# Layer 0's modulation by pool groups on 32-column TensorE tiles, with the mixer in turned form

## The chip, the core and the metric

The kernel runs on one core of one Trainium2 chip. The metric is the device time of one execution in microseconds, the median of several runs. Engines are named as in the profile: PE (TensorE), PEld (its weight loads), DVE (VectorE), ACT (ScalarE), POOL (GpSimd), SP (SyncE, which issues most DMAs).

## What is computed

A decoder trunk of two layers on a sequence of 256 tokens and 2048 channels, all in float32. Layer 0 mixes by causal window means, layer 1 by attention; each layer ends in a gated FFN of 5632 hidden channels. Shift, scale and gate of each sub-layer come from a vector `c`, through `mod_w[i]` (2048 x 12288, 100 MB a layer). The part that the change touches, cut:

```python
shift_m, scale_m, gate_m, shift_f, scale_f, gate_f = jnp.split(silu(c) @ mod_w[0] + mod_b[0], 6, axis=-1)
h = rmsnorm(x, norm_mix[0]) * (1 + scale_m) + shift_m
for g, w in enumerate((2, 4, 8, 16)):           # four groups of 512 channels
    d_g = causal window mean over w tokens of h_g, less h_g
    y_g = d_g @ pool_w[0, g]                    # 512 x 512
x = x + gate_m * (y * pool_scale[0])
h = rmsnorm(x, norm_ffn[0]) * (1 + scale_f) + shift_f
x = x + gate_f * swiglu(h, ffn_gate[0], ffn_up[0], ffn_down[0])
```

## The kernel before

**Units.** Weights of the big products come as units of 512 x 512 (1 MB). `w_unit` loads one, ACT rounds it to a high part (line 368), DVE takes the low part (line 370), and PE multiplies high and low parts with the two parts of the hidden state (`proj_unit`, line 392). The product with `silu(c)` has a single row, so before it is done mostly on DVE: `Part.unit` loads 128 rows of 2048 columns (1 MB, rows of 8 KB) and adds them, scaled, to `acc` (line 183); `BlockPart.unit` does it for 512 columns of shift and of scale at once (two loads of 512 KB in pieces of 2 KB, line 219; sums at line 233). Sums over partitions are then made by PE.

**Front.** Before the first FFN product, layer 0 needs shift, scale and gate of the mixer whole (48 loads of 1 MB) and the first quarter of the FFN's shift and scale (16 loads of 512 KB), `x`, the band matrices and the four pool weights (1 MB each). The order is: shift of the mixer, scale of the mixer, and between them the window products of the normed stream (lines 716 to 728); then pool weights, gate, and the products with pool weights (`pool_product`, line 784). Of the gate's 16 row tiles five go to PE (`GM_PE`, line 200), the rest to DVE. Then `add_gated` adds the gated result to `x` (lines 525 and 526), the squares are summed over the free axis on ACT (line 410), POOL takes the power -0.5 of two columns (line 415), and the first quarter of the hidden state is scaled, turned by PE (line 444) and modulated (lines 458 to 460). Of the first block of the FFN's shift and scale half of the rows are summed on PE (line 230) and the rest on DVE, and PE folds them into columns (line 247).

**What sets the order.** The units of modulation lie in a list, `background`; `pump` emits the next ones. In the FFN one unit of weights is followed by a share of a unit of background. SP issues in the order of the program and waits for one of six `raw` buffers; each engine runs its instructions in order. The front from the modulation of the window means to the first hidden block stands in `manual_schedule`, so it runs as written; elsewhere a scheduler with priorities orders the instructions.

**First FFN.** `start_ffn` begins six chunks of gate and up block by block of the hidden state; blocks 1 to 3 are scaled on ACT (line 434), turned on PE and modulated while PE works on the block before. At chunk 5 the stream `x` is written to DRAM (`stream_aside`, 2 MB, line 482) and the tile gathers the FFN's sum.

Of the kernel before, what the change touches and what calls it, by code (L numbers as in the profile page):

```python
# [9 lines left out]
F32 = mybir.dt.float32  # L10
# [37 lines left out]
C_END = C_FOLD + P  # L48
# [9 lines left out]
GM_PE = (8, 10, 12, KD - 2, KD - 1)  # L58
# [8 lines left out]
V_NM, V_NF, V_KVIN, V_KVN, V_QN, V_C, V_END = 0, 32, 64, 80, 84, 88, 104  # L67


def shape_constants():  # L70
# [8 lines left out]
    con[:, C_SIGN] = np.where(q % ROPE < HALF, -1.0, 1.0)  # L79
    band = np.zeros((P, len(WINDOWS), BAND_W), np.float32)  # L80
# [12 lines left out]
def tile_trunk(ctx: ExitStack, tc: tile.TileContext, a: dict, out: bass.AP):  # L93
# [34 lines left out]
    # constants and small vectors  # L128
    x = const.tile([P, NT, D], F32, name="x")

    def load_x(tok):
        sync.dma_start(x[:, tok, :], a["x"][0, tok * P:(tok + 1) * P, :])
# [22 lines left out]
    sync.dma_start(vrows[V_QN:V_QN + 4], a["q_norm"].rearrange("l (r q) -> (l r) q", q=P))  # L155
    vps = ps_t()
    pe.transpose(vps[:, :V_END], vrows, ident[:V_END, :V_END])
    vcol = const.tile([P, V_C], F32, name="vcol")
    dve.tensor_copy(vcol, vps[:, :V_C])
# [3 lines left out]
    # adaLN rows: acc[p, n] = sum over row tiles of w[kt*128+p, n] * silu(c); partition 0 starts at the bias  # L163
# [22 lines left out]
    # a gate on all partitions, with some of its row tiles summed on the idle tensor engine  # L186
    class SharedPart(Part):
        def add(self, r):
            if self.kt == 0:
                self.banks = [ps_t() for _ in range(ND)]  # L190
            if self.kt not in GM_PE:
                super().add(r)
                return
            rep = t2k([P, P])
            act.activation(rep, ones, AF.Copy, scale=s_col[:, self.kt:self.kt + 1])
            for j in range(ND):
                js = slice(j * CH, (j + 1) * CH)
                if self.kt == KD - 1:
                    pe.matmul(self.banks[j], lhsT=ones, rhs=self.acc[:, js], start=False, stop=False)
                pe.matmul(self.banks[j], lhsT=rep, rhs=r[:, js], start=self.kt == GM_PE[0], stop=self.kt == KD - 1)  # L200

    # the same for CH columns of shift and scale at once, two row tiles in a unit
    class BlockPart:
        def __init__(self, w, b, col, done, shared):
            self.w, self.b, self.col, self.done, self.shared, self.kt = w, b, col, done, shared, 0
            self.banks = None

        def unit(self):
            pick = slice(self.col, self.col + CH)
            if self.kt == 0:  # L210
                self.acc = work.tile([P, 2, CH], F32, tag="acc", bufs=2, name=nm("acc"))
                pool.memset(self.acc, 0.0)
                sync.dma_start(self.acc[0:1], self.b.rearrange("o (i n) -> o i n", i=2)[:, :, pick])
                if self.shared:
                    self.banks = [ps_t() for _ in range(2)]
# [4 lines left out]
            if self.shared and self.kt == KD - 2:  # L220
                self.sums = ps_t()
                for i in range(2):
                    row = t2k([P, CH])
                    act.activation(row[0:1, :], self.banks[i][0:1, :], AF.Copy)
                    self.add_sums(i, row[0:1, :], ones[0:1, 0:1], i == 0, False)
            for k in range(2):
                s_ = s_col[:, self.kt + k:self.kt + k + 1]
                if self.shared and k == 1 and self.kt < KD - 2:
                    for i in range(2):
                        pe.matmul(self.banks[i][0:1, :], lhsT=s_, rhs=r[:, k, i, :], start=self.kt == 0,  # L230
                                  stop=self.kt == KD - 4)
                else:
                    dve.scalar_tensor_tensor(out=self.acc, in0=r[:, k], scalar=s_, in1=self.acc,  # L233
                                             op0=ALU.mult, op1=ALU.add)
            self.kt += 2
            if self.kt == KD and self.shared:
                for i in range(2):
                    self.add_sums(i, self.acc[:, i], ones[:, 0:1], False, i == 1)
                self.done(self.sums)
            elif self.kt == KD:  # L240
                self.done(self.acc)

        def add_sums(self, i, rows, ones_, first, last):
            """Adds the sums over partitions of rows [..., CH] to KL columns of a bank, which only its first product clears."""
            for k in range(KL):
                n = i * KL + k
                pe.matmul(self.sums[:, n:n + 1], lhsT=rows[:, k * P:(k + 1) * P], rhs=ones_, start=first and k == 0,
                          stop=last and k == KL - 1)
# [3 lines left out]
    def folded(acc, n, fin):  # L252
        """Sums over partitions of acc [P, n]: column 32 * b + i is in row 32 * r + i of column b, for any r."""
# [17 lines left out]
    def to_cols(fin):  # L271
        def done(acc):
            pt = ps_t()
            for j in range(KD):
                pe.matmul(pt[:, j:j + 1], lhsT=acc[:, j * P:(j + 1) * P], rhs=ones[:, 0:1], start=True, stop=True)  # L275
            fin(pt[:, :KD], slice(0, P))
        return done

    def shift_to(i, form=to_cols_folded):
        return form(lambda pt, rows: dve.tensor_copy(cols[rows, i, :], pt))  # L280

    def scale_to(i, g, form=to_cols_folded):
        return form(lambda pt, rows: dve.scalar_tensor_tensor(
# [42 lines left out]
    # units of the background for a unit of weights  # L326
# [4 lines left out]
    def hold():  # L331
        """Emit no more of the background until release()."""
# [14 lines left out]
    def plan(left, units):  # L347
        """Spread the background down to what is left over the next units of weights."""
# [4 lines left out]
    # what follows a unit of weights, queued behind the split of the next unit, which is more pressing  # L353
# [9 lines left out]
    # weights: a unit of 512 rows and 512 columns, split exactly into two parts of 12 bits  # L363
# [23 lines left out]
    def proj_unit(banks, t_, hi, lo, first, last, toks=range(NT)):  # L387
        """Adds a unit to the banks; the products with the lower part of the weights, which is split last, come last."""
# [13 lines left out]
    # statistics of the residual stream  # L402
# [5 lines left out]
    def stat_piece(tok, j):  # L408
        junk = work.tile([P, CH], BF16, tag="junk", bufs=1, name=nm("junk"))
        act.activation(junk, x[:, tok, j * CH:(j + 1) * CH], AF.Square, accum_out=ssq[0][:, tok, j:j + 1])  # L410
# [68 lines left out]
    def stream_aside(l):  # L479
        aside[l] = dram.tile([P, NT, D], F32, name=nm("aside"))  # L480
# [53 lines left out]
    # a projection of the hidden state, begun before all of the hidden state is known  # L534
# [109 lines left out]
    # rope tables with the rows of two heads on partitions; the sine has the sign of its half  # L644
# [32 lines left out]
    def rope_start(bank):  # L677
        """bank [128, T] holds the rows of two heads; returns what rope_end needs."""
# [13 lines left out]
    rope_tables()  # L692
    load_x(1)
    band = hl_t([P, len(WINDOWS), BAND_W], F32)
    sync.dma_start(band, a["band"].rearrange("p (g n) -> p g n", g=len(WINDOWS)))
    psc = hl_t([P, D], F32)
    ps_row = t2k([P, CH])
    for j in range(ND):
        sync.dma_start(ps_row[j * 32:j * 32 + 1, :], a["pool_scale"][0:1, j * CH:(j + 1) * CH])
    for j in range(ND):  # L700
        pt = ps_t()
        pe.matmul(pt, lhsT=ones[j * 32:j * 32 + 1, :], rhs=ps_row[j * 32:j * 32 + 1, :], start=True, stop=True)
        act.activation(psc[:, j * CH:(j + 1) * CH], pt, AF.Copy)
    stat_start()
    for tok in range(NT):
# [413 lines left out]
```

## Time and profile before

| what | us |
|---|---|
| median of 3 runs | 1964.37 (1963.92 to 1965.63) |
| span of the profiled execution | 1962.3 |
| last loads of the front have landed (66.3 MB) | about 172.7 |
| first product of the first FFN | 184.3 |
| PE busy in the whole span | 1853.0 |

The profile comes from one profiled execution; its span runs from the first to the last instruction, and the time of a run holds what lies around it too. The profile's views give, for a stretch, the busy time of each engine and how many instructions it ran; for a group, the count, the busy time, the mean length of one and the idle time ahead of it; for DMA, the bytes and the rate.

### The profile page before, as it was taken

The numbers are of one execution on the slowest core, as the hardware profiler recorded it, in microseconds if no ns is written. First come the engines' busy times: TensorE is split into PE (matmuls) and PEld (weight loads), VectorE is DVE, ScalarE is ACT, GpSimd is POOL, SyncE is SP. The second block draws the span as 40 slices with busy tenths as digits, with TensorE's granted clock in tenths as the row PEclk, the third lists the DMA queues.
The fourth block names the chain that finished last, engine by engine and source line by source line (L and its number), as shares of the span: only waits on it lengthen the run. The fifth ranks groups of instructions, "written<-read, shape, count | busy, mean of one in ns | idle before, by whom it ended". The sixth has DMA issues, their size and how long they took to land. (4 is left out here: it accounts for less than half of the span.)

```text
span 1962.3 us, 21516 instructions
## 1 busy us (share of the span) xinstructions
PE 1853.0 (94%) x8485; PEld 1520.7 (77%) x8485; DVE 1546.4 (79%) x1312; ACT 850.0 (43%) x939; POOL 35.9 (2%) x33
## 2 busy tenths in 40 slices
PE   0489999999999999998999999999999999999998
PEld 0444888888888888886789987888888888888886
DVE  7887899998778778888989975889986566554556
ACT  3123544444443333334676744544444433343333
POOL 1000000000000000000000000000000000000000
PEclk9889999999999999999899999999999999999999
DMA  9999998898898989987888684989887667665561
GB/s 377 408 378 365 379 321 305 310 350 327 313 329 302 332 325 345 338 333 284 307 311 304 228 295 142 360 303 325 297 293 260 225 229 257 235 209 186 195 219 70
DMA packets 225184, 572.66 MB, mean 292 GB/s; under 512 B 11958, under 2 KB 16286, under 8 KB 203442
## 3 DMA queue, kind: packets, MB, share of 16 engines
q1 hardware_dynamic: 225084, 571.30, 80.9%
q8 instruction: 66, 1.08, 0.2%
q14 instruction: 34, 0.28, 0.0%
HBM read 564.97 MB, written 6.29 MB: 291 GB/s over the span
## 5 line engine op out<-in xcount | busy, mean ns | idle before, releaser
L392 PE MATMUL ps<-hl,act 128*128 128x512 f32 x7008 | 1609.5, 391 | 4.7 <-ACT act L459 2.2
L392 PEld LDWEIGHTS ps<-hl,act 128*128 128x128 f32 x7008 | 1315.1, 188 | 279.3 <-ACT act L459 4.4
L370 DVE TENSOR_TENSOR hl<-raw,hl 128x2048 fp32r<-128x2048 f32 x296 | 676.2, 2289 | 239.9 <-ACT hl L368 236.1
L368 ACT ACTIVATE hl<-raw 128x2048 fp32r<-128x2048 f32 x296 | 566.4, 1919 | 608.7 <-PE ps L392 542.1
L183 DVE SCALAR_TENSOR_TENSOR acc<-raw,s_col,acc 128x2048 f32<-128x2048 f32 x155 | 364.0, 2348 | 4.2 <-DMA raw<-in_mod_w_dram 1.6
L233 DVE SCALAR_TENSOR_TENSOR acc<-raw,s_col,acc 128x1024 f32<-128x1024 f32 x121 | 155.0, 1281 | 8.7 <-DMA raw<-in_mod_w_dram 7.2
L556 DVE TENSOR_TENSOR act<-ps,act 128x512 f32<-128x512 f32 x96 | 64.6, 687 | 14.1 <-PE ps L392 13.7
L275 PE MATMUL ps<-ones,acc 128*128 128x1 f32 x64 | 13.9, 352 | 62.8 <-DVE acc L183 39.9
L410 ACT ACTIVATE junk<-x 128x512 bf16<-128x512 f32 x40 | 25.2, 630 | 89.6 <-DVE x L526 44.1
L275 PEld LDWEIGHTS ps<-ones,acc 128*128 128x128 f32 x64 | 13.8, 332 | 64.5 <-DVE acc L183 41.4
L590 ACT ACTIVATE act<-ps 128x512 fp32r<-128x512 f32 x44 | 23.8, 596 | 61.5 <-PE ps L587 53.4
L625 DVE TENSOR_TENSOR x<-ps,x 128x512 f32<-128x512 f32 x32 | 22.1, 691 | 35.4 <-PE ps L392 35.4
L458 ACT ACTIVATE t2k<-ps,cols 128x256 f32<-128x256 f32 x64 | 33.2, 567 | 21.6 <-PE ps L444 17.0
L634 ACT ACTIVATE t2k<-ps 128x512 f32<-128x512 f32 x24 | 14.2, 593 | 64.2 <-PE ps L392 64.2
L918 PE MATMUL ps<-act,hl 128*128 128x256 f32 x128 | 37.2, 291 | 0.6 <-DVE hl L370 0.6
L919 PE MATMUL ps<-act,hl 128*128 128x256 f32 x128 | 36.7, 287 | 0.0
L920 PE MATMUL ps<-act,hl 128*128 128x256 f32 x128 | 36.1, 286 | 0.0
L591 DVE TENSOR_TENSOR act<-ps,act 128x512 fp32r<-128x512 f32 x44 | 28.2, 685 | 8.1 <-ACT act L590 8.0
L638 DVE TENSOR_TENSOR t2k<-ps,t2k 128x512 f32<-128x512 f32 x24 | 16.6, 690 | 21.3 <-PE ps L392 21.3
L444 PE MATMUL ps<-con,t2k 128*128 128x128 f32 x144 | 22.5, 306 | 11.2 <-DVE t2k L432 8.1
L784 PE MATMUL ps<-act,act 128*128 128x512 f32 x64 | 30.7, 644 | 0.9 <-issue 0.9
L554 ACT ACTIVATE act<-ps 128x512 f32<-128x512 f32 x32 | 19.1, 598 | 28.3 <-PE ps L392 28.1
(168 smaller groups left out, 955.0 us busy)
## 6 DMA issues: line engine op xcount, KB each, us to landing
raw<-in_mod_w_dram SPq DMA_DIRECT2D x128, 1024.0 KB
raw<-in_ffn_gate_dram SPq DMA_DIRECT2D x88, 1024.0 KB
raw<-in_ffn_up_dram SPq DMA_DIRECT2D x88, 1024.0 KB
raw<-in_ffn_down_dram SPq DMA_DIRECT2D x88, 1024.0 KB
raw<-in_mod_w_dram SPq DMA_DIRECT2D x128, 512.0 KB
raw<-in_kv_mod_w_dram SPq DMA_DIRECT2D x32, 1024.0 KB
raw<-in_w_o_dram SPq DMA_DIRECT2D x16, 1024.0 KB
raw<-in_w_uq_dram SPq DMA_DIRECT2D x8, 768.0 KB
```

The source lines that it names most:

```text
L183: dve.scalar_tensor_tensor(out=self.acc, in0=r, scalar=s_col[:, self.kt:self.kt + 1], in1=self.acc, op0=ALU.mult, op1=ALU.add)
L233: dve.scalar_tensor_tensor(out=self.acc, in0=r[:, k], scalar=s_, in1=self.acc, op0=ALU.mult, op1=ALU.add)
L368: hi_ins = act.activation(hi, r, AF.Copy)
L370: lo_ins = dve.tensor_tensor(out=lo, in0=r, in1=hi.bitcast(F32), op=ALU.subtract)
L392: pe.matmul(banks[tok], lhsT=t_[:, i, k, tok * P:(tok + 1) * P], rhs=w[:, k, :], start=first and n < len(part), stop=last and n >= len(ord ...
L458: act.activation(full, pts[k // 2][:, k % 2, :], AF.Identity, scale=scale, bias=bias)
L556: dve.tensor_tensor(out=part, in0=banks[tok], in1=part, op=ALU.add)
L591: dve.tensor_tensor(out=m[:, 1, :, ts_], in0=v, in1=m[:, 0, :, ts_].bitcast(F32), op=ALU.subtract)
L784: pe.matmul(pt, lhsT=pooled[g // 2][:, g % 2, k, tok * P:(tok + 1) * P], rhs=wp[g][:, k, :], start=k == 0, stop=k == KL - 1)
L918: pe.matmul(pt[:, h, :], lhsT=wl(h0 + h, k), rhs=t_[:, 0, k, :], start=k == 0, stop=False)
L919: pe.matmul(pt[:, h, :], lhsT=wh(h0 + h, k), rhs=t_[:, 0, k, :], start=False, stop=False)
L920: pe.matmul(pt[:, h, :], lhsT=wh(h0 + h, k), rhs=t_[:, 1, k, :], start=False, stop=k == KL - 1)
```

## The change

The front of layer 0 is written anew; from the second FFN unit on the program is the same but for the hidden blocks 1 to 3 of the first FFN.

* **Strips.** Modulation of mixer and gate is no longer summed on DVE. `s_strip` holds `silu(c)` as the first of 32 columns for each row tile. A unit (`Strips.unit`) loads 1 MB, either two row tiles of 512 columns of shift and scale (two loads of 512 KB) or four row tiles of 512 columns of the gate (four of 256 KB), all in pieces of 2 KB. PE multiplies each piece of 128 x 512 with a stationary tile of 128 x 32 whose output stands on partitions 0, 32, 64 or 96 of one bank; a bank gathers 16 row tiles. `columns` copies the bank to SBUF (ACT), and four small products with a selection matrix (`C_SEL`) sum the strips and turn them into columns.
* **Order.** The loads go by pool group: 8 units of shift and scale and 4 of the gate for group 0, then group 1, and so on, and at the end 8 units of the FFN's first block: 56 units. `then(n, f)` says what is emitted behind unit n. All of it stands in `manual_schedule`.
* **Turned mixer.** `x` is turned at the start (16 x 2 transposes), the window means and the products with pool weights are made in turned form, and `mix_in` adds the gated result to the turned stream, which lives in the tile of `x`. The pool scale is folded into the gate's columns.
* **Norm.** `mix_total` sums the squares over channels on PE, into a bank that holds the same 256 sums on all partitions; `norm_total` scales them on DVE, and POOL takes the power -0.5 of 128 x 256 into the tile of the rope key. `hidden_T` multiplies the turned stream with it, on DVE, for all four blocks; no transposes follow, and `halves_T` modulates.
* **Stream aside.** `turn_back` transposes each group back, and ACT issues its writes to DRAM in the front (8 of 256 KB); `stream_aside(0)` does nothing.

```diff
-class SharedPart(Part): ...
+class Strips:
+    def unit(self):
+        if self.kt == 0:
+            self.bank = ps_t()
+        r = raw_t([P, self.rows, self.n, CH])
+        for k in range(self.rows):
+            sync.dma_start(r[:, k], self.w[:, self.kt + k])
+        for m in range(NSTRIP):
+            k, i = m // self.n, m % self.n
+            pe.matmul(self.bank[m * STRIP:(m + 1) * STRIP, :], lhsT=s_strip[:, self.kt + k, :], rhs=r[:, k, i, :],
+                      start=self.kt == 0, stop=self.kt + self.rows == KD)
+        self.kt += self.rows
+        if self.kt == KD:
+            self.done(self.columns())
...
+def mix_total(g):
+    for k in range(KL):
+        pe.matmul(total[:, :T], lhsT=ones, rhs=squares[g][k // 2][:, k % 2, :], start=g == 0 and k == 0,
+                  stop=g == ND - 1 and k == KL - 1)
+def turn_back(g):
+    for tok in range(NT):
+        pt = ps_t()
+        for k in range(KL):
+            pe.transpose(pt[:, k * P:(k + 1) * P], xT[:, g * KL + k, tok * P:(tok + 1) * P], ident)
+        piece = t2k([P, CH])
+        act.activation(piece, pt, AF.Copy)
+        act.dma_start(aside[0][:, tok, g * CH:(g + 1) * CH], piece)
+def norm_total():
+    v = t2k([P, T])
+    dve.tensor_scalar(out=v, in0=total[:, :T], scalar1=1.0 / D, scalar2=EPS, op0=ALU.mult, op1=ALU.add)
+    pool.tensor_tensor(out=rstd_b, in0=v, in1=mhalf[:, 0:1].to_broadcast([P, T]), op=ALU.pow)
+def hidden_T(j):
...
+        dve.tensor_tensor(out=both[:, k % 2, :], in0=xT[:, j * KL + k, :], in1=rstd_b, op=ALU.mult)
...
+for g in range(ND):
+    n = len(units)
+    units += [strip_cols(0, 2, g, mix_cols)] * (KD // 2)
+    then(n + 6, load_pool_w, g)
+    then(n + 7, pool_modulate, g)
+    units += [strip_cols(2, 1, g, gate_cols)] * (KD // 4)
+    for q in range(4):
+        then(n + 8 + q, pool_product, g, q)
+    then(n + 12, mix_in, g)
+    then(n + 13, mix_total, g)
+    then(n + 14, turn_back, g)
+    if g == ND - 1:
+        then(n + 14, norm_total)
+for i in range(2 * ND):
+    then(i + 1, pool_half, i // 2, i % 2)
+n = len(units)
+units += [strip_cols(3, 2, 0, ffn_cols)] * (KD // 2)
...
+then(n + 5, lambda: first.append(hidden_T(0)))
+then(n + 5, lambda: w_early(ffn_weights(0)[GATE][0:CH, 0:CH]))
```

Where instructions stand, at two places. First PE, at the end of the front, before: the last row sums of the FFN's first block (line 230), the transposes of the first hidden block (line 444), the folds (line 247), and the first FFN product (line 392).

```order
L230 MATMUL ps_589<-raw_676,s_col 1x512
L444 MATMUL ps_682<-con,t2k_666 128x128
L444 MATMUL ps_682<-con,t2k_668 128x128
...
L247 MATMUL ps_695<-ones,t2k_696 128x1 x4
L247 MATMUL ps_695<-ones,t2k_702 128x1 x4
L247 MATMUL ps_695<-ones,acc_585 128x1 x8
L392 MATMUL ps_749<-hl_722,act_726 128x512
```

The same place now: strips (line 229 of the changed kernel), sums of squares (832), transposes back (842), the fold of the last strips (242) and the first FFN product (402).

```order
L229 MATMUL ps_961<-raw_977,front 32x512 x4
L832 MATMUL ps_109<-t2k_973,ones 128x256 x2
L832 MATMUL ps_109<-t2k_975,ones 128x256 x2
L229 MATMUL ps_961<-raw_988,front 32x512 x4
L842 MATMUL ps_995<-con,x 128x128 x4
L842 MATMUL ps_1003<-con,x 128x128 x4
...
L229 MATMUL ps_961<-raw_1054,front 32x512 x4
L242 MATMUL ps_1063<-con,t2k_1061 128x2 x4
L402 MATMUL ps_1090<-hl_1043,act_1071 128x512
```

The sums of squares stand behind the second of the last eight units, the transposes of the hidden block are gone, and behind the last strips only a fold stands ahead of the FFN.

Second DVE, the same stretch, before: the sum of squares and its scaling (lines 420 and 414), the two multiplications with POOL's power (432), the last sums of modulation (233), the FFN's shift and scale (737 and 738), the split of the first FFN weights (370).

```order
L420 TENSOR_REDUCE sm_660<-ssq_584 128x2
L414 TENSOR_SCALAR sm_663<-sm_660 128x2
L432 TENSOR_SCALAR t2k_666<-x,rstd_662 128x512
L432 TENSOR_SCALAR t2k_668<-x,rstd_662 128x512
...
L233 SCALAR_TENSOR_TENSOR acc_585<-raw_692,s_col,acc_585 128x1024 x2
L737 COPY cols<-ps_695 128x4
L738 SCALAR_TENSOR_TENSOR cols<-ps_695,vcol 128x4
L370 TENSOR_TENSOR hl_723<-raw_720,hl_722 128x2048
```

Now: the last gated addition (822), the scaling (849), the four multiplications with POOL's power, which lies in `krT` (857), the split (380), and then the FFN's shift and scale (750 and 752).

```order
L822 SCALAR_TENSOR_TENSOR x<-ps_934,front,x 128x256 x2
L849 TENSOR_SCALAR t2k_1011<-ps_109 128x256
L857 TENSOR_TENSOR t2k_1035<-x,krT 128x256 x2
L857 TENSOR_TENSOR t2k_1038<-x,krT 128x256 x2
L380 TENSOR_TENSOR hl_1044<-raw_1041,hl_1043 128x2048
L750 TENSOR_TENSOR cols<-ps_1063,front 128x4 x2
L752 TENSOR_TENSOR cols<-cols,vcol 128x4
```

The multiplications now stand ahead of the split and of the last shift and scale, so all three kinds are queued behind POOL's power.

More of the change, by code (lines that the diff above doesn't have):

```diff
@@ L219, in unit @@
                 sync.dma_start(r[:, k], rows[:, k, :, pick])
[L220 to L225, printed above, removed]
-            for k in range(2):
[L227 to L234, printed above, removed]
-            self.kt += 2
[L236 to L240, printed above, removed]
-                self.done(self.acc)
[L243 to L248, printed above, removed]
+            for k in range(2):
+                dve.scalar_tensor_tensor(out=self.acc, in0=r[:, k], scalar=s_col[:, self.kt + k:self.kt + k + 1],
+                                         in1=self.acc, op0=ALU.mult, op1=ALU.add)
+            self.kt += 2
+            if self.kt == KD:
+                self.done(self.acc)
     pending = []
@@ L269, in to_cols_folded, with shift_to, scale_to @@
         return lambda acc: folded(acc, D, fin)
[L271 to L283, printed above, removed]
+    def shift_to(i):
+        return to_cols_folded(lambda pt, rows: dve.tensor_copy(cols[rows, i, :], pt))
+    def scale_to(i, g):
+        return to_cols_folded(lambda pt, rows: dve.scalar_tensor_tensor(
             out=cols[rows, i, :], in0=pt, scalar=1.0, in1=vcol[rows, g:g + KD], op0=ALU.add, op1=ALU.mult))
@@ L758, in start_ffn @@
                     if n == 2 * len(begun) - 1:
-                        hT.append(modulated(turned_pieces(pieces), j + 1, cscale, cshift))
+                        hT.append(hidden(j + 1, pieces))
                     begun[c][which].block(j, hT[j])
                     if n == 2 * len(begun) - 5:
-                        pieces = scaled(rstd, j + 1)
+                        pieces = ahead(j + 1)
                     if todo:
@@ new lines, in tile_trunk @@
+    pool_all = [act_t([P, 2, KL, T], F32) for _ in range(2)]
+    rope_tables()
+    stat_start()
+    for tok in range(NT):
+        for j in range(ND):
+            stat_piece(tok, j, xn[tok])
+    rstd = stat_finish()
+    with tc.manual_schedule():
+        for n, part in enumerate(units):
+            part.unit()
+            for f, args in after.get(n, ()):
+                f(*args)
+        first = halves_T(0, first[0])
+    for j in range(1, ND):
+        push(sf_block(0, j, C_SF0, C_AF0), KD // 2)
```

267 lines of the change are left out of this document (151 added, 116 removed).

## The prediction

> **What bounds the kernel now.** I read the span in stretches first: what each engine did from the start to the last loads of layer 0's modulation (172.7 us), from there to the first product of the first FFN (184.3), and from the dense run (187.5) to its end. Columns: length, busy time of PE, weight loads, DVE, ACT and POOL, granted clock, DMA share, GB/s.
>
> ```profile
> 20.00:140.00 120.00, 59.53 (x208) 40.86 (x208) 102.92 (x63) 20.91 (x43) 2.76 (x2) 0.86 1.01 411
> 140.00:150.00 10.00, 9.02 (x22) 3.90 (x21) 6.42 (x6) 2.06 (x6) 0.00 (x0) 1.00 0.64 241
> 150.00:172.70 22.70, 22.70 (x54) 7.20 (x54) 16.39 (x21) 5.79 (x16) 0.95 (x1) 1.00 1.02 365
> 172.70:184.30 11.60, 7.85 (x45) 5.76 (x43) 7.65 (x12) 4.10 (x6) 1.65 (x2) 0.85 1.05 389
> 187.50:1953.00 1765.50, 1747.68 (x8146) 1460.27 (x8146) 1397.52 (x1179) 799.67 (x833) 24.89 (x17) 0.99 0.80 282
> ```
>
> From 187.5 us on PE is busy for 1747.7 of 1765.5 us: that part is TensorE's and the change leaves its products alone. The front before it is the DMA queues' (share about 1), but for a dip at 140 to 150 us. So the whole is the moment when the first FFN begins plus a fixed run. PE's waits after that moment are few, the longest groups these:
>
> ```profile
> PE ps L444 <- DVE t2k L432: 8.1, 2, 4.1
> PE ps L392 <- ACT hl L368: 1.9, 1, 1.9
> ```
>
> Then the timeline, for how that moment comes about (start, length):
>
> ```profile
> 174.70 5.24 DVE L233 SCALAR_TENSOR_TENSOR acc<-raw,s_col,acc 128x1024 f32<-128x1024 f32 x4
> ...
> 180.00 2.90 PE L247 MATMUL ps<-ones,acc 128*128 128x1 f32 x16 [2.30 <-DVE acc L233]
> 184.32 3.03 PE L392 MATMUL ps<-hl,act 128*128 128x512 f32 x6 [1.43 <-ACT act L459]
> 187.50 12.79 PE L392 MATMUL ps<-hl,act 128*128 128x512 f32 x55
> ```
>
> The sums on DVE end at 179.9, PE folds them, and ACT's first hidden block lets PE go at 184.3. The DMA view up to 172.7 us gives the bytes, two more stretches the rate:
>
> ```profile
> DMA packets 14248, 66.27 MB, mean 384 GB/s; under 512 B 1238, under 2 KB 1470, under 8 KB 7840
> ```
>
> ```profile
> DMA packets 1291, 6.24 MB, mean 312 GB/s; under 512 B 189, under 2 KB 421, under 8 KB 681
> ```
>
> ```profile
> DMA packets 3996, 29.07 MB, mean 415 GB/s; under 512 B 449, under 2 KB 449, under 8 KB 449
> ```
>
> ```profile
> DMA packets 6502, 12.64 MB, mean 383 GB/s; under 512 B 337, under 2 KB 337, under 8 KB 6501
> ```
>
> The second is the first 20 us; the third (20 to 90 us) mostly whole rows of 8 KB, the fourth (157 to 190 us) almost all pieces of 2 KB. All that layer 0's front must load is 66.3 MB (48 loads of 1.05 MB, 8.4 MB for the FFN's first shift and scale, 4.2 of pool weights, 3.3 of the rest), so the last of it lands at about 172.7 us, and 11.6 us pass until the first product.
>
> **The change part by part.** *Loads.* The same 58.7 MB of modulation now come in pieces of 2 KB, so I price them at 383 GB/s and not at 415; the gate's loads are of 256 KB, half of any in that row, and could be slower (365 at worst, the lowest stretch above without a dip). Ahead of the last two units SP now issues the first FFN weights (1.05 MB), and ACT writes the stream aside (2.1 MB, until now in the FFN). To land: 66.3 + 1.05 + 2.1 = 69.4 MB. With the 6.24 MB of the first 20 us as before, 63.2 / 0.383 = 165 us, so 185 us; some small loads that stood ahead of the first large one are gone, which I put at 1 us: **184**. The dip is gone too: in its place the 6 buffers are freed by PE.
>
> *PE in the front.* Each MB takes four matmuls of 32 columns, and a float matmul is two passes. What passes cost, by group:
>
> ```profile
> L200 PE MATMUL ps<-raw,t2k 128*128 128x512 f32 x40 | 18.1, 595 | 1.0 <-ACT t2k L195 1.0
> L230 PE MATMUL ps<-raw,s_col 128*1 128x512 f32 x28 | 12.2, 592 | 0.0
> L275 PE MATMUL ps<-ones,acc 128*128 128x1 f32 x64 | 13.9, 352 | 62.8 <-DVE acc L183 39.9 <-issue 22.9
> L726 PE MATMUL ps<-hl,t2k 128*128 128x256 f32 x32 | 10.8, 424 | 0.0
> L727 PE MATMUL ps<-hl,t2k 128*128 128x128 f32 x32 | 6.6, 292 | 0.0
> L784 PE MATMUL ps<-act,act 128*128 128x512 f32 x64 | 30.7, 644 | 0.9 <-issue 0.9
> ```
>
> 14 products of 512 columns with one output column are 28 passes in 12.2 us, 0.43 us each. One after the other, eight are 3.5 us a MB against 2.7 of DMA; with four tiles side by side two rounds, 0.87, say 1.0. No column tiles stand in the trace, but tiles of another kind do: four products with one row each, on rows 0, 32, 64 and 96:
>
> ```profile
> L702 PE MATMUL ps<-t2k,ones x8: 1052/1120/1217, 14.2 to 15.7; 1*128 1x512 f32 x8
> ```
>
> Eight passes of over 1 us each start within 1.5 us, so tiles do run together; I take 1.0 us, 56 in all. The Trainium skill (TensorE: Matmul & The Clock Gate, Part 3) says that a weight load overlaps running matmuls only where the row group differs, and column tiles all have the same rows; yet it reports 2.38 times for three column tiles. By the first sentence the sum would be nearer the 3.5 us. No run here shows it.
>
> The rest of PE's front: window products as before (L726 and L727, 17.4), products with pool weights 27.5 at the full clock (L784: 64 passes of 0.43, now 128 of half the length), nine folds of 8 passes at 0.22, 64 transposes at 0.11 (below), sums of squares 32 × 0.215: some 75 us. With 56 it is 131 of 184, so hidden behind the loads.
>
> *The end of the front.* After the last landing: strip 1.0, copy 0.6, fold 1.8, three small DVE operations 0.5, ACT's first block 1.0, handing over 0.5: 5.4 us in place of 11.6, of rows like these (and L275):
>
> ```profile
> L786 ACT ACTIVATE act<-ps 128x512 f32<-128x512 f32 x8 | 4.8, 598 | 22.9 <-PE ps L784 22.9
> ```
>
> ```profile
> 182.93 0.16 DVE L737 COPY cols<-ps 128x4 f32<-128x4 f32 x1 [2.99 <-PE ps L247]
> 183.00 0.15 DVE L738 SCALAR_TENSOR_TENSOR cols<-ps,vcol 128x4 f32<-128x4 f32 x1
> ...
> 183.25 0.56 ACT L458 ACTIVATE t2k<-ps,cols 128x256 f32<-128x256 f32 x1 [4.29 <-DVE cols L738]
> 183.85 0.42 ACT L459 ACTIVATE act<-t2k 128x256 fp32r<-128x256 f32 x1
> ```
>
> First product at 184 + 5.4 = 189.4: 5.1 later than 184.3.
>
> *The norm.* POOL's power now works on 128x256, once, where it was 128x2. Its rows:
>
> ```profile
> L415 POOL TENSOR_TENSOR rstd<-sm,mhalf 128x2 f32<-128x2 f32 x4 | 2.8, 696 | 106.9 <-DVE sm L414 96.3 <-DMA raw<-in_mod_w_dram 10.6
> L415 POOL TENSOR_TENSOR sm<-sm,mhalf 128x2 f32<-128x2 f32 x2 | 5.5, 2746 | 100.7 <-DVE sm L414 100.7
> L473 POOL TENSOR_TENSOR sm<-sm,mhalf 128x1 f32<-128x1 f32 x2 | 1.1, 552 | 613.0 <-DVE sm L472 613.0
> ```
>
> ```profile
> L183 DVE SCALAR_TENSOR_TENSOR acc<-raw,s_col,acc 128x2048 f32<-128x2048 f32 x43 | 101.1, 2352 | 3.0 <-DMA raw<-in_mod_w_dram 0.5
> ```
>
> The two of 2.75 us run beside a sum of 2.35 us on DVE (L183), which stands still here; I leave them out. Between the others a second column costs 0.144 us. If each does, 256 take 0.55 + 255 × 0.144 = 37.3 us; if it is mostly a fixed cost, about 1 us: those are the ends. It starts when the sums of squares stand, after unit 49 of 56; behind that unit 7.9 MB are still to land (six units, weights, half a MB written), 20.5 us, less 3.5 for strip, eight passes, DVE and handing over: 17 us before the last landing. Up to 17 us are hidden; 37.3 end 20.3 us after the landing. DVE waits for it in its order, and behind that wait stand the four multiplications, the split of the first FFN weights, and the three operations that make the last shift and scale:
>
> ```profile
> L370 DVE TENSOR_TENSOR hl<-raw,hl 128x2048 fp32r<-128x2048 f32 x296 | 676.2, 2289 | 239.9 <-ACT hl L368 236.1
> L670 DVE TENSOR_TENSOR t2k<-t2k,t2k 128x256 f32<-128x256 f32 x1 | 0.4, 416 | 0.0
> ```
>
> 20.3 + 4 × 0.42 + 2.29 + 0.5 + 1.0 + 0.4 = 26.2 us after landing in place of 5.4: 20.8 more. I take the long end, since the only two sizes in the trace differ by that slope.
>
> *In the FFN.* Three blocks of 8 transposes leave PE's dense run:
>
> ```profile
> 1279.81 0.87 PE ps L444 x8
> ```
>
> 3 × 0.87 = 2.6 us gained. DVE gets 12 more multiplications of 0.42 there; PE's waits above show slack for most, 0 to 2 us, I take 0.5. The write aside leaves SP's queue: nothing, PE does not wait for it.
>
> *Sum,* against the span of 1962.3, which lies 2.1 under the median of 1964.4: 5.1 + 20.8 - 2.6 + 0.5 = +23.8, 1988 us.
>
> **Rivals.** *The power is short* (0.32): all but the sum's 20.8 us stays, +3.0, 1967; with 365 to 400 GB/s 1960 to 1976. For it: two points of 128x1 and 128x2 say little of a long loop. The Trainium skill (GPSIMD Engine Reference, Performance versus the Vector engine) has 4497 ns for an addition of 2048 columns, 2.2 ns a column; by it the power would be some 1 us. No run here shows a long one.
>
> *The loads keep the pace of whole rows* (0.10), with a short power; the other side: 63.2 / 0.415 = 152, landing at 171, product at 176.7, 7.6 earlier, less 2.6: 1954. It decides below zero from 400 GB/s. Against it: 383 in the row of 2 KB pieces, which lasts 33 us.
>
> *Tiles one after the other* (0.08): 448 passes × 0.43 = 193 us and 75 more on PE from 14 us on, with bubbles first product near 292: about 2070. L702 speaks against it. The Trainium skill's sentence on weight loads (TensorE: Matmul & The Clock Gate, Part 3) would point to this case; no run here shows it.
>
> *The power is long* (0.50): 1988, with 365 to 400 GB/s 1980 to 1996.
>
> **The numbers.** I predict the likeliest, 1988. The range from 1958 to 1996 takes in the long and the short power with their rates and leaves out the tiles one after the other and most of the fast loads. About 0.2% (3.9 us) is what can be told from no change. Faster: 0.10 and a quarter of the short power, 0.18; same: 0.14; slower: 0.50 + 0.08 + 0.10 = 0.68.
>
> **What would show it.** Right: one POOL operation of 30 to 40 us, DVE idle until it ends, PE's first FFN product at about 210 us, DMA still for some 15 us before. Wrong in the power: it lasts under 17 us and the first product is near 189. Wrong in the rate: over 400 GB/s between 20 and 170 us. Wrong in the tiles: eight passes of a unit over 2 us, and loads that wait for PE. Wrong altogether: the dense run after the first product longer or shorter by more than 3 us.

## The result and the profile after

| | before | after |
|---|---|---|
| median, us | 1964.84 (1963.92 to 1965.63, 4 runs) | 2008.16 (2005.74 to 2010.91, 4 runs) |
| ratio, 95% interval | | 1.0221, 1.0207 to 1.0236 |
| span of the profiled execution, us | 1962.3 | 2008.0 |
| first product of the first FFN, us | 184.3 | 232.5 |
| from there to the end of the span, us | 1778.0 | 1775.5 |

The change is slower by 43 us. By the spans, the FFN begins 48.2 us later and the fixed run behind it is 2.5 us shorter. So the whole loss is in the front, as forecast, but it is nearly twice the 24 us of the forecast, and 2008 lies outside the range. The runs of one kernel spread with the granted clock of TensorE: in the changed kernel from 2005.74 us at 0.981 to 2010.91 us at 0.974.

The changed kernel in stretches (length, busy time of PE, weight loads, DVE, ACT and POOL, clock, DMA share, GB/s):

```profile
20.00:140.00 120.00, 99.05 (x565) 52.56 (x564) 18.14 (x56) 23.88 (x44) 0.00 (x0) 0.90 0.99 363
140.00:150.00 10.00, 10.00 (x71) 4.56 (x69) 1.75 (x4) 2.45 (x4) 0.00 (x0) 1.00 1.05 386
150.00:172.70 22.70, 14.93 (x54) 5.76 (x51) 2.07 (x7) 2.30 (x5) 0.00 (x0) 0.70 0.92 329
172.70:184.30 11.60, 10.80 (x67) 6.14 (x66) 2.08 (x6) 1.86 (x3) 0.00 (x0) 1.00 1.05 386
184.30:210.00 25.70, 13.37 (x71) 4.34 (x69) 0.43 (x1) 3.70 (x4) 23.79 (x1) 0.78 0.96 345
210.00:232.50 22.50, 0.01 (x1) 0.01 (x1) 3.96 (x9) 1.08 (x3) 18.30 (x2) 0.50 0.04 11
```

Two things are seen. In the last row POOL runs alone until its power ends at 227.3 us: PE is busy for 0.01 of 22.5 us and the queues move 11 GB/s. And further up the rate is 386 GB/s in two rows, about what 2 KB pieces were priced at, but only 329 to 363 in the others. The end of the front in the timeline (start, length, and in brackets the idle time ahead and what ended it):

```profile
185.71 0.43 DVE L849 TENSOR_SCALAR t2k<-ps 128x256 f32<-128x256 f32 x1 [2.90 <-PE ps L832]
186.21 41.14 POOL L850 TENSOR_TENSOR krT<-t2k,mhalf 128x256 f32<-128x256 f32 x1 [169.25 <-DVE t2k L849]
...
203.13 1.05 PE L242 MATMUL ps<-con,t2k 128*128 128x2 f32 x8 [0.70 <-ACT t2k L238]
227.39 1.43 DVE L857 TENSOR_TENSOR t2k<-x,krT 128x256 f32<-128x256 f32 x4 [41.25 <-POOL krT L850]
228.74 2.28 DVE L380 TENSOR_TENSOR hl<-raw,hl 128x2048 fp32r<-128x2048 f32 x1
230.94 0.22 DVE L750 TENSOR_TENSOR cols<-ps,front 128x4 f32<-128x4 f32 x2
...
232.49 1.74 PE L402 MATMUL ps<-hl,act 128*128 128x512 f32 x3 [28.30 <-ACT act L867]
```

The power takes 41.1 us. PE folds the last strips at 203.1, and from then on all waits for POOL. Behind the power stand on DVE, as listed in the prediction, the four multiplications, the split and the small operations: 5.1 us from POOL's end to the first product.

The second part of the loss is in the loads. Stretches of 6 us around the moments at which ACT writes the stream:

```profile
66.00:72.00 6.00, 6.00 (x48) 2.83 (x50) 0.00 (x0) 1.19 (x2) 0.00 (x0) 1.00 1.01 352
72.00:78.00 6.00, 1.14 (x12) 0.13 (x4) 0.00 (x0) 0.00 (x0) 0.00 (x0) 0.83 0.46 150
102.00:108.00 6.00, 6.00 (x44) 2.87 (x40) 0.00 (x0) 1.20 (x3) 0.00 (x0) 1.00 1.05 388
108.00:114.00 6.00, 3.65 (x19) 0.58 (x16) 0.00 (x0) 0.00 (x0) 0.00 (x0) 1.00 0.67 248
144.00:150.00 6.00, 6.00 (x46) 2.51 (x44) 0.00 (x0) 1.19 (x2) 0.00 (x0) 1.00 1.04 385
150.00:156.00 6.00, 2.69 (x12) 0.29 (x8) 0.00 (x0) 0.00 (x0) 0.00 (x0) 1.00 0.55 160
186.00:192.00 6.00, 4.52 (x40) 1.64 (x32) 0.14 (x1) 1.19 (x2) 5.79 (x1) 1.00 1.05 389
192.00:198.00 6.00, 1.65 (x6) 0.33 (x8) 0.00 (x0) 1.91 (x1) 6.00 (x1) 0.79 0.67 221
```

Four times the rate falls to 150 to 250 GB/s for a stretch. The waits of SP's queue name what it stood for (total, times, longest):

```profile
SPq L226 <- DMA aside<-t2k: 18.4, 3, 9.1
SPq L795 <- DMA aside<-t2k: 17.7, 2, 9.5
```

In the front SP issues loads only, and yet it waits for the writes of the stream, which ACT issues. At the first of the four places SP stands still from 66.2 to 75.75, ACT issues its writes at 69.85 and 70.87, and SP goes on when the first has landed (SP's queue, then ACT's):

```profile
65.75 0.47 SPq L795 DMA_DIRECT2D act<-in_pool_w_dram  x1
75.75 4.27 SPq L226 DMA_DIRECT2D raw<-in_mod_w_dram  x8
```

```profile
69.85 0.34 ACTq L845 DMA_DIRECT2D aside<-t2k  x1
```

The list of the built program says why. SP's and ACT's DMAs share eight semaphores, DMAHW0 to DMAHW7, handed out in turn, and each DMA waits for the one that had its semaphore before. Here the load in row 63 comes after the first write on DMAHW0 (its wait on DMAHW2 is for the earlier load into its buffer):

```
ACT  40 L845 DMA aside_110<-t2k_481 128x512 [waits DMAHW0_49,Activation_49]
ACT  42 L845 DMA aside_110<-t2k_489 128x512 [waits DMAHW2_49,Activation_49]
SP   62 L795 DMA act_520<-in_pool_w_dram 128x4x512 [waits DMAHW7_49]
SP   63 L226 DMA raw_522<-in_mod_w_dram 128x2x512 [waits DMAHW2_49,DMAHW0_49,PE_49]
```

With six buffers SP is up to six units ahead of PE, but the write is issued only when PE has turned the group back. So eight DMAs on, SP stands until PE, ACT and the write have caught up, and meanwhile what is queued runs dry. In all four groups the load that stalled is the next on the semaphore of that group's first write.

### The profile page after: what moved, and what is told of

Read it like the earlier page. It is cut to its first block, busy times and chain, and to the rows that moved or that the text cites. A ratio compares the mean times of both kernels' runs of the same rounds, so it can differ in the third digit from the quotient of the medians.

```text
span 2008.0 us, 22476 instructions
## 1 busy us (share of the span) xinstructions
PE 1899.2 (95%) x8954; PEld 1532.1 (76%) x8954; DVE 1438.6 (72%) x1303; ACT 845.9 (42%) x919; POOL 68.7 (3%) x30
## 5 line engine op out<-in xcount | busy, mean ns | idle before, releaser
L210 DVE SCALAR_TENSOR_TENSOR acc<-raw,s_col,acc 128x2048 f32<-128x2048 f32 x112 | 262.6, 2344 | 1.0 <-DMA raw<-in_mod_w_dram 0.6
L262 DVE SCALAR_TENSOR_TENSOR acc<-raw,s_col,acc 128x1024 f32<-128x1024 f32 x112 | 143.2, 1279 | 2.3 <-DMA raw<-in_mod_w_dram 1.0
L229 PE MATMUL ps<-raw,front 128*32 128x512 f32 x448 | 76.4, 667 | 36.1 <-DMA raw<-in_mod_w_dram 36.1
L229 PEld LDWEIGHTS ps<-raw,front 128*32 128x32 f32 x448 | 12.3, 113 | 72.5 <-DMA raw<-in_mod_w_dram 49.7
L850 POOL TENSOR_TENSOR krT<-t2k,mhalf 128x256 f32<-128x256 f32 x1 | 41.1, 41140 | 169.2 <-DVE t2k L849 169.2
L238 ACT ACTIVATE t2k<-ps 128x512 f32<-128x512 f32 x9 | 5.4, 597 | 89.1 <-PE ps L229 89.1
L421 ACT ACTIVATE junk<-x 128x512 bf16<-128x512 f32 x24 | 15.1, 629 | 60.2 <-DVE x L519 40.0
L813 PEld LDWEIGHTS ps<-act,act 128*128 128x128 f32 x128 | 26.3, 216 | 15.9 <-issue 7.7
L647 ACT ACTIVATE t2k<-ps 128x512 f32<-128x512 f32 x24 | 14.2, 591 | 54.8 <-PE ps L402 54.8
L813 PE MATMUL ps<-act,act 128*128 128x256 f32 x128 | 36.9, 438 | 0.3 <-DVE act L803 0.3
L651 DVE TENSOR_TENSOR t2k<-ps,t2k 128x512 f32<-128x512 f32 x24 | 16.6, 690 | 28.4 <-PE ps L402 28.4
```

Of the source, the lines that this page charges most:

```text
L210: dve.scalar_tensor_tensor(out=self.acc, in0=r, scalar=s_col[:, self.kt:self.kt + 1], in1=self.acc, op0=ALU.mult, op1=ALU.add)
L229: pe.matmul(self.bank[m * STRIP:(m + 1) * STRIP, :], lhsT=s_strip[:, self.kt + k, :], rhs=r[:, k, i, :], start=self.kt == 0, stop=self.kt ...
L813: pe.matmul(mixed[g][-1][:, n % 2, :], lhsT=wp[g][:, k, ns], rhs=pool_all[g // 2][:, g % 2, k, :], start=k == 0, stop=k == KL - 1)
L850: pool.tensor_tensor(out=rstd_b, in0=v, in1=mhalf[:, 0:1].to_broadcast([P, T]), op=ALU.pow)
```

## The experiments

The theory was: (A) POOL's power sets the first product, about 25 us; (B) SP's waits for the writes set the last landing, up to 17 us. The rivals were that either is the whole loss, or that the bytes of the writes or the size of the loads make them late. Line numbers in the rows are those of the kernel shown.

**Power of two columns.** The sums are taken out of the bank with the identity, POOL takes the power of 128x2, and two products with ones spread it again.

```diff
-        pool.tensor_tensor(out=rstd_b, in0=v, in1=mhalf[:, 0:1].to_broadcast([P, T]), op=ALU.pow)
...
+        for tok in range(NT):
+            dve.tensor_tensor(out=own[:, tok], in0=total[:, tok * P:(tok + 1) * P], in1=ident, op=ALU.mult)
+        dve.tensor_reduce(out=ss, in_=own, axis=AX.X, op=ALU.add)
+        dve.tensor_scalar(out=v, in0=ss, scalar1=1.0 / D, scalar2=EPS, op0=ALU.mult, op1=ALU.add)
+        pool.tensor_tensor(out=r, in0=v, in1=mhalf, op=ALU.pow)
+        for tok in range(NT):
+            dve.tensor_scalar(out=spread[0][:, tok], in0=ident, scalar1=r[:, tok:tok + 1], scalar2=None, op0=ALU.mult)
...
+    # behind the next unit
+            pe.matmul(pt[:, tok * P:(tok + 1) * P], lhsT=ones, rhs=spread[0][:, tok], start=True, stop=True)
+        act.activation(rstd_b, pt[:, :T], AF.Copy)
```

> The power -0.5 is taken of 2 columns (the sums are picked out by the identity, POOL takes the power of 128x2, two products with ones spread it over the partitions); all else as in the changed kernel. Theory A (POOL's power of 41.1 us sets the first FFN product, SP's waits for the writes of the stream set the last landing, about 201 us): the last landing stays at about 201, the first product comes at about 207 in place of 232.5, the time is 2008 - 25 = 1983. Rival (the power is the whole loss, the loads are late only because POOL and DVE stand still): landing near 186, first product near 192, 1968. Rival (the power was hidden, the loads alone are late): no change, 2008.

Measured: 1980.8 us (ratio to before 1.0076, 1.0060 to 1.0092), 27 less than the changed kernel. PE at the end of this kernel's front:

```profile
193.13 3.74 PE L229 MATMUL ps<-raw,front 128*32 128x512 f32 x12
197.57 1.05 PE L242 MATMUL ps<-con,t2k 128*128 128x2 f32 x8 [0.70 <-ACT t2k L238]
200.22 0.73 PE L402 MATMUL ps<-hl,act 128*128 128x512 f32 x2 [1.60 <-ACT act L882]
```

The fold is followed by the first product within 2.7 us. The rival that the power is all (1968) falls, the one that it was hidden (2008) too. The first product is 32.3 us earlier, not 25: the fold itself came 5.6 us sooner, since SP's longest waits at the third and fourth place were 6.3 and 6.5 us here and 9.5 and 9.1 in the changed kernel.

The traces show where that difference comes from. Behind the second stall PE has little to do (from 114 to 118 us it is busy for 0.59 us in the changed kernel and 1.19 here), and from 118 to 122 us its granted clock is 0.50 in both kernels; from there to 130 us it stays at 0.50 in the changed kernel, while here it is 0.81 and then 1.00. The third group's first product with its pool weights, in the changed kernel and then here:

```profile
127.28 3.61 PE L813 MATMUL ps<-act,act 128*128 128x256 f32 x8
```

```profile
126.17 1.99 PE L813 MATMUL ps<-act,act 128*128 128x256 f32 x8 [0.32 <-DVE act L803]
```

So PE turns the group back later, ACT reaches the group's first write at 147.5 us in the changed kernel and at 144.8 here, and SP waits that much longer for it. The fourth place looks alike: from 160 to 170 us the clock is 0.50 there, 0.89 and 1.00 here. A stall can thus lengthen the next one.

**Writes from POOL's queue.** The same writes at the same places, the power long as in the change.

```diff
-            act.dma_start(aside[0][:, tok, g * CH:(g + 1) * CH], piece)
+            pool.dma_start(aside[0][:, tok, g * CH:(g + 1) * CH], piece)
```

> The eight writes of the stream are issued by POOL in place of ACT; the same bytes at the same places, the power stays 128x256. Theory (SP's loads wait for these writes by way of a shared place in the queues): the four stalls of SP of 9 to 10 us go, the last landing is near 186 in place of 201; the power starts some 11 us earlier, less about 3 us for POOL's two last issues, ends near 219, the first product is near 224, the time 1999 to 2000. Rival (the bytes of the writes, 2.1 MB, and the rate of small loads are what costs): landing stays near 201, and the power starts 3 us later: 2011.

Measured: 2005.0 us (1.0199, 1.0184 to 1.0214). The stretch from 20 to 180 us, in the changed kernel and then here:

```profile
20.00:180.00 160.00, 130.49 (x723) 66.69 (x721) 21.97 (x67) 29.23 (x54) 0.00 (x0) 0.88 0.99 360
```

```profile
20.00:180.00 160.00, 136.82 (x794) 69.17 (x792) 24.45 (x74) 31.25 (x58) 6.96 (x9) 0.94 1.05 384
```

No wait of SP for a write is left, with the same bytes written. In the list of this program POOL's writes stand on semaphores of their own, DMASW0 to DMASW7, and no load of the front waits for one. PE and POOL then:

```profile
190.61 1.05 PE L242 MATMUL ps<-con,t2k 128*128 128x2 f32 x8 [0.76 <-ACT t2k L238]
223.86 2.67 PE L402 MATMUL ps<-hl,act 128*128 128x512 f32 x5 [32.20 <-ACT act L867]
```

```profile
176.38 1.16 POOL L845 DMA_DIRECT2D aside<-t2k  x2 [34.14 <-ACT t2k L844]
177.55 41.17 POOL L850 TENSOR_TENSOR krT<-t2k,mhalf 128x256 f32<-128x256 f32 x1
```

The last fold is 12.5 us earlier (190.6 for 203.1); the power starts 8.7 earlier and again ends last, so the first product gains 8.6, as the theory has it. Of that the span keeps 6.8 and the median 3.1, less than the 8 to 9 expected, with runs from 2002.8 to 2008.4. The interval of the ratio overlaps that of the changed kernel (1.0207 to 1.0236), so by the medians alone this gain is not clear; the traces show it, and the next run.

**Both.**

> Power of 2 columns and the writes issued by POOL, together. Theory (two causes that add up): 64.0 MB after the first 20 us at 385 GB/s, last landing near 186, first product near 191.5, 1967, a little over the kernel before. Rival (writes cost by their bytes): landing near 201, 1983. Rival (something else holds the loads too): in between.

Measured: 1974.2 us (1.0039, 1.0025 to 1.0053). SP no longer waits for writes, 383 GB/s from 20 to 180 us, and PE:

```profile
189.36 1.05 PE L229 MATMUL ps<-raw,front 128*32 128x512 f32 x4 [0.30 <-DMA raw<-in_mod_w_dram]
191.17 1.05 PE L242 MATMUL ps<-con,t2k 128*128 128x2 f32 x8 [0.76 <-ACT t2k L238]
193.82 0.73 PE L402 MATMUL ps<-hl,act 128*128 128x512 f32 x2 [1.60 <-ACT act L882]
```

Both causes are shown, each with the other gone: stalls 6.6 us (1980.8 to 1974.2), power 30.9 (2005.0 to 1974.2). Expected was 1967; the last landing is at 189 and not 186. To the kernel before 8.4 us are left (1974.2 for its 1965.8 in the same session): the last loads land 16.6 us later (189.3 for 172.7), the end of the front is 7.1 shorter (4.5 for 11.6), so the first product is 9.5 later, and about 1 us comes back behind it.

**The power by size.** Six powers and a multiplication were put on POOL at the start. I had taken POOL to be idle there, but the power of the first norm queues behind them, so this kernel is late as a whole (2070.2 us, one run) and only its durations are used.

> The changed kernel with six more powers on POOL at the start, where POOL is idle, of 1, 2, 16, 64, 128 and 256 columns, and one multiplication of 256 columns; the output is the same. Theory (a fixed part and a price per column): 0.55, 0.70, 2.9, 10.6, 21 and 41 us. Rival (short loops are cheap, long ones go in blocks): not on a line, 256 columns far over twice 128. The multiplication, if POOL's elementwise work as such is slow: over 10 us; if it is the power: under 1 us. The time stays at 2008, since POOL has nothing else to do there.

```profile
L914 POOL TENSOR_TENSOR krT<-krT,mhalf 128x256 f32<-128x256 f32 x1 | 41.1, 41115 | 0.1
L914 POOL TENSOR_TENSOR krT<-krT,mhalf 128x128 f32<-128x128 f32 x1 | 20.7, 20725 | 0.1
...
L914 POOL TENSOR_TENSOR krT<-krT,mhalf 128x16 f32<-128x16 f32 x1 | 2.9, 2904 | 0.1
...
L915 POOL TENSOR_TENSOR krT<-krT 128x256 f32<-128x256 f32 x1 | 0.6, 612 | 0.1
L914 POOL TENSOR_TENSOR krT<-krT,mhalf 128x1 f32<-128x1 f32 x1 | 0.6, 552 | 0.1
```

A straight line: (41115 - 552) / 255 = 159 ns a column. It is the power and not POOL: a multiplication of 256 columns takes 0.61 us.

**The writes put off to the FFN.** As with the power of two columns, but the pieces stay in SBUF and SP writes them in the FFN.

```diff
-            act.dma_start(aside[0][:, tok, g * CH:(g + 1) * CH], piece)
...
+            act.activation(kept[tok][:, g * CH:(g + 1) * CH], pt, AF.Copy)
...
+    # behind the second and third unit of background
+            sync.dma_start(aside[0][:, NT - self.n], kept[NT - self.n])
```

> Power of 2 columns, and the stream turned back is kept in SBUF in the front and written by SP in two pieces of 1 MB behind the second and third unit of modulation in the FFN, where the kernel before had its write. Theory (what is left of the loss in the run with both mended, 1974, is bytes ahead of the first product: 3.1 MB more to land than before): 2.1 MB less ahead of it, landing 188 - 5.5 = 182.5, first product near 188.5, and the FFN takes the write as before: 1968 to 1970. Rival (the rest of the loss is not bytes but the rate of small pieces or PE's work): 1974.

Measured: 1974.7 us (1.0043, 1.0029 to 1.0057): no gain, though the last strips start at 182.8 and the first product stands at 187.3, as the theory has it for the front. The 76 us from there, and the 71 us from the first product on of the kernel with both mended, about 300 products each:

```profile
187.30:263.70 76.40, 71.61 (x303) 56.96 (x304) 65.72 (x65) 42.57 (x48) 2.44 (x3) 0.98 1.02 374
```

```profile
193.80:264.50 70.70, 70.47 (x303) 57.28 (x303) 65.58 (x65) 42.88 (x48) 1.48 (x2) 0.98 1.04 378
```

Of the 6.5 us won, 5.7 are given back in these stretches (76.4 us for 70.7): PE is idle for 4.8 us among the first products here, 0.2 there. ACT's waits for the FFN's weights in the same stretches, here and then with both mended, tell why:

```profile
ACT hl L378 <- DMA raw<-in_ffn_gate_dram: 15.7, 4, 8.2
ACT hl L378 <- DMA raw<-in_ffn_up_dram: 11.0, 3, 6.0
```

```profile
ACT hl L378 <- DMA raw<-in_ffn_up_dram: 3.5, 1, 3.5
ACT hl L378 <- DMA raw<-in_ffn_gate_dram: 1.8, 1, 1.8
```

The FFN begins under full queues (DMA share 1.02 and 1.04), so bytes moved from the front into its beginning are only moved.

**The writes three units later in the program**, still from ACT, power of two columns.

```diff
-            act.dma_start(aside[0][:, tok, g * CH:(g + 1) * CH], piece)
+            back[g, tok] = piece
...
+    def write_back(g):
+        for tok in range(NT):
+            act.dma_start(aside[0][:, tok, g * CH:(g + 1) * CH], back[g, tok])
...
+        then(n + 17, write_back, g)
```

> Power of 2 columns; ACT still issues the writes of the stream, but they stand three units later in the program. Theory (a load of SP waits for the write that stands up to eight DMAs ahead of it in the program, so what counts is that ACT reaches the write before SP reaches that load): the stalls of SP shrink from 6 to 10 us to under 3, landing near 189, 1974 to 1976. Rival (ACT's queue or the writes themselves slow the loads): as with the writes where they were, 1981.

Measured: 1979.1 us (1.0069, 1.0055 to 1.0082), a miss: 34.1 us of SP's waits for the writes remain. In the built list the writes moved by a load or less and not by three units: the build hands out the semaphores in an order of its own, and ACT's queue still has each write right behind its copies. The first write had DMAHW1 in place of DMAHW0, and the stall came exactly one load later: the load that had waited until 75.75 was issued at 66.65, and the next, on DMAHW1, at 75.84. At the second and third place the wait moved as well, from the pool weights (L795) to the load behind them (L226). So the edit did not do what it should, but it confirms which load waits.

**One load per MB of the gate**, beside the writes put off.

```diff
+            if self.n == 1:
+                sync.dma_start(r[:, :, 0], self.w[:, self.kt:self.kt + self.rows, 0])
```

> As the run with the stream kept in SBUF, and each MB of the gate is one load in place of four of 256 KB. Theory (the queues are full, the rate is set by pieces of 2 KB): the same within 1 us, 1968 to 1970. Rival (the size of a load costs): 16 MB at more than 386 GB/s, up to 3 us faster.

Measured: 1973.9 us (1.0046, 1.0033 to 1.0060), against 1974.7 no difference, and the first product is no earlier (189.1 for 187.3). Loads of 256 KB cost nothing here.

**Strips alone, in the kernel before.** The first block of the FFN's shift and scale goes through strips; all else stays as before.

```diff
-                if self.shared and k == 1 and self.kt < KD - 2:
-                    for i in range(2):
-                        pe.matmul(self.banks[i][0:1, :], lhsT=s_, rhs=r[:, k, i, :], ...)
+                for i in range(2):
+                    if self.shared:
+                        m = 32 * (2 * k + i)
+                        pe.matmul(self.bank[m:m + 32, :], lhsT=s_strip[:, self.kt + k, :], rhs=r[:, k, i, :],
+                                  start=self.kt == 0, stop=self.kt == KD - 2)
```

> The kernel before, with strips of 32 columns for the first block of the FFN's shift and scale alone (8 units, all rows on PE, none on DVE). Theory (column tiles are the part of the change that pays: strips, copy, fold and two DVE operations end 5 to 6 us after the last landing in place of 11.6): first product at 178 to 180, faster by 4 to 6 us, 1960 to 1962. Rival (the split of the first FFN weights, whose load lands last, ends the front in any case): no change, 1965.8.

Measured: 1960.7 us (ratio 0.9976, 0.9966 to 0.9985, 9 runs): faster than both kernels, and 4.8 us faster than the kernel before (1965.5 in the same session). The end of its front:

```profile
172.87 2.08 PE L235 MATMUL ps<-raw,krT 128*32 128x512 f32 x8
175.64 1.95 PE L254 MATMUL ps<-krT,t2k 128*128 128x1 f32 x16 [0.70 <-ACT t2k L243]
179.43 4.83 PE L399 MATMUL ps<-hl,act 128*128 128x512 f32 x9 [1.85 <-ACT act L466]
```

First product at 179.4 in place of 184.3: the short tail behind the last landing is the part of the change that pays.

**The gate in strips as well**, on top of that: whole rows of 8 KB, one strip for each chunk of 512 columns, the products with pool weights between the units.

```diff
+            for j in range(ND):
+                pe.matmul(self.bank[32 * j:32 * j + 32, :], lhsT=s_strip[:, self.kt, :], rhs=r[:, j * CH:(j + 1) * CH],
+                          start=self.kt == 0, stop=self.kt == KD - 1)
...
+            pump((3, 3, 2, 2)[g])
-        pump(10)
```

> As the run with strips for the FFN's first block in the kernel before, and the mixer's gate in strips too: 16 units of whole rows of 8 KB, each column chunk on a strip of its own, four row products at the end that spread the gate over the partitions; no sums of the gate on DVE, and the products with pool weights stand between the units. Theory (the loads stand still at 140 to 150 us, 252 GB/s there, because DVE frees the buffers late): the dip goes, landing and first product 3 to 4 us earlier, 176, and 1957. Rival (the products with pool weights, 30 us of PE, hold the strips and so the buffers): the dip only moves, 1960 to 1963.

Measured: 1965.6 us (1.0002, 0.9993 to 1.0011): the rival's side, and beyond it.

```profile
121.25 7.13 PE L798 MATMUL ps<-act,act 128*128 128x512 f32 x16
128.31 2.78 PE L207 MATMUL ps<-raw,krT 128*32 128x512 f32 x24
```

PE works without a gap, 7.1 us of pool products ahead of every few units, and SP waits 36.9 us for it to free the buffers. From 120 to 150 us the queues move 285 GB/s on average, 350 in the kernel without this edit, and the first product is at 184.1 in place of 179.4. DVE's wait was exchanged for one for PE.

## Why the prediction was wrong

The direction and the mechanism that decides (the long power) were right; the time was 20 us short of the measured one. By steps, on the profiled executions:

* **Loads, last landing 184: this step failed.** In the changed kernel the last strips could start at 200.6 only (the row below, their weight loads). The rate itself was right: 383 forecast, 385 to 389 where nothing stalls. Two things were missing. Without stalls the landing is at 189.3 (the kernel with both mended), 5.3 later than forecast. The last strips of the changed kernel, then the DMA view of the kernel with both mended for its first 20 us, and up to its landing:

```profile
200.55 0.19 PEld L229 LDWEIGHTS ps<-raw,front 128*32 128x32 f32 x4 [1.44 <-DMA raw<-in_mod_w_dram]
```

```profile
DMA packets 2078, 5.43 MB, mean 272 GB/s; under 512 B 238, under 2 KB 566, under 8 KB 1822
```

```profile
DMA packets 35665, 70.32 MB, mean 371 GB/s; under 512 B 2713, under 2 KB 3041, under 8 KB 35399
```

The first 20 us brought 5.4 MB and not 6.24 (2.1 us), 0.9 MB more than the 69.4 had landed (2.4 us), and the 1 us taken off for small loads did not come. The other 11 us are the stalls: by the four low rows above, 24 us at 150, 248, 160 and 221 GB/s in place of 386 leave 4.6 MB behind, by this estimate 12 us at 386. The step priced "ACT writes the stream aside" as 2.1 MB, and the last part said of the write "nothing, PE does not wait for it". PE does not, but SP does, and SP's loads are what the front is made of. The write left SP's queue, but not the chain of semaphores in which SP's loads wait.
* **PE's strips:** 1.0 us a MB forecast, tiles side by side. In the changed kernel eight passes start to end in 1.07 us (the x8 row below), against 3.5 us one after the other. So the rival with serial tiles is out. The Trainium skill's sentence that a weight load overlaps only where the row group differs (TensorE: Matmul & The Clock Gate, Part 3) pointed to that rival; these tiles all have the same rows, and no such delay is seen. The gain that the Trainium skill reports in the same section, 2.38 times for three column tiles, is the better guide. The four here gain 3.3 times (3.5 us against 1.07).

```profile
185.60 1.07 PE L229 MATMUL ps<-raw,front 128*32 128x512 f32 x8
```

* **The end of the front:** 5.4 us from the last landing to the first product; 4.5 from the last strips in the kernel with both mended. Right.
* **The norm:** the slope from one to two columns, 0.144 us, gave 37.3 us; it took 41.1 (0.159 a column), 3.8 more. The two sizes in the trace were enough for the mechanism, but their difference carries 10% of error. The Trainium skill's figure for POOL (GPSIMD Engine Reference, Performance versus the Vector engine), 2.2 ns a column for an addition, fits the multiplication here (2.4) and not the power, which is some 65 times as dear.
* **First product 210:** it came at 232.5. The power started at 186.2 and not at 167 (19.2: landing 16.5, and 2.7 less work left behind its start), it lasted 3.8 longer, and 5.1 instead of 5.9 us followed it: 22.2 together.
* **The FFN:** 2.1 us gained by forecast, 2.5 between the two profiled executions. That is about what executions differ by: from the first product on, the kernel with strips alone, whose FFN is that of before, takes 1780.6 us, and the kernel before 1778.0. The list of PE's waits leaves out one of 3.0 us in layer 1 (L885), which changes no term.

What stays open: why PE's clock came back sooner behind the second stall in one kernel than in the other, and why the writes from POOL's queue moved the median by less than the first product. The later landing that is left without stalls was not split further into bytes, rate and the first 20 us by runs of their own, but for the 2.1 MB of the writes. That a wait of SP for ACT's writes disappears with another semaphore on the same queue of ACT was not tried.

## What to carry to other kernels

Ask of every DMA that is moved to another engine which later DMAs wait for it, and when its own engine will reach it; a write that waits for computation must not share the in-order chain of loads that run ahead of that computation. A function that costs little on a column can cost its price per column on a tile: take it on the small form and spread the result, as two products on PE did here. And what is taken off a stage bound by loads is gained only if the next stage isn't bound by loads as well.

## What the runs showed that was not expected

* POOL's power of 128 partitions costs 159 ns a column on a straight line from 1 to 256 columns, its multiplication 2.4.
* Four column tiles of 32 run eight passes of 512 in 1.07 us (24 passes in 2.78 in the last run), where a pass by itself takes 0.43.
* A stall of the loads can lengthen the next one: with PE's granted clock at 0.50 behind it, eight passes took 3.61 us in place of 1.99, and the write that the next load waits for came 2.7 us later.
* Pieces of 2 KB land at the same pace whether the gate's loads are of 256 KB or of 1 MB (1974.7 and 1973.9 us for the whole).
